# Low parts of the weights: stored to device memory at their first use, loaded from there at the second

## The chip, the cores and the metric

The kernel runs on one core of one Trainium2 chip. The metric is the time of one execution on the device in microseconds (us); lower is better. A core has five engines that run side by side, each with its own queue worked off in order: TensorE (PE, matrix products; its weight loads are shown apart as PEld), VectorE (DVE), ScalarE (ACT), GpSimd (POOL) and SyncE (SP), which here issues all DMA transfers. An instruction that waits holds up everything behind it in its engine's queue.

## The reference, cut to what matters

A decoder trunk of two layers works on a sequence of 1024 tokens with 1024 channels. In each layer the normalized input goes through one wide projection whose columns feed four mixers (a sparse attention, a gated spatial unit, a convolution module, a linear recurrence); their results go through an output projection, are normalized and added to the stream, and then a gated embedding is added:

```python
for i in range(DEPTH):
    h = rms_norm(x, g_pre[i])
    proj = h @ w_in[i]                      # 1024 x 3532, split among the mixers
    ...
    mix = concatenate([y_a * silu(z_a), y_b * silu(z_b), y_c * silu(z_c), y_d * silu(z_d)])
    x = x + rms_norm(mix @ w_out[i], g_post[i])
    x = x + sigmoid(x @ ple_gate[i]) * (p[i] @ ple_proj[i])
```

All is in float32. What the change touches are the four weight matrices `w_in`, `w_out`, `ple_gate` and `ple_proj`, which every token is multiplied with.

## The kernel before, in words

**Products in three parts.** Float32 products are made from a rounded format (`F32R`). A weight and an activation are each split into a high part (the value rounded to that format) and a low part (what the rounding left over); `mm3` (L161 to L165) then makes three products, high x high (L163), high x low (L164) and low x high (L165).

**Granules.** The weights stream through SBUF in granules of at most 128 x 512 numbers (256 KB). `w_granule` (L167) names the rows and columns, and `split_w` (L149) does the work: SP loads the raw numbers into a buffer `ws` (L154), ACT rounds them into `wh` (L157), and POOL subtracts the two into `wl` (L158). `ws`, `wh` and `wl` have three buffers each. There are 388 granules in the whole program; PE works 12 matrix products on most of them, 6 on a few.

**Halves.** The sequence is worked in two halves of 512 tokens (`h` 0 and 1) within each layer (`l` 0 and 1). Each half streams the layer's weights anew, so most granules are loaded and split twice. The string `ORDER` lists the steps of each (layer, half): `F`, `N`, `G`, `a` to `d` and `s` stream `w_in`, `O` streams `w_out` of the half before, `g` its `ple_gate`, `e` streams `ple_proj`; `R` and `r` are the recurrence, `A` a tile of attention, `T` the 31 convolution taps on DVE (L688). The granules number 64, 96, 96 and 132 in the four (layer, half) stages in program order; the last has the tail with it. `tail` (from L1134) ends the program for the last half: it cuts `w_out` and half of `ple_gate` into other granules than the steps `O` and `g` do.

**What sets the order.** The framework plans the program when it is built: it simulates the engines with its own costs and due times, fills each engine's queue in the order that comes out, and adds the semaphore waits. `split_w` runs under a raised priority (`high_priority(offset=4000)`), so that granules are fetched as early as their three buffers allow. A buffer is given to the next tile when the last instruction that uses it has ended.

Other transfers on the same SP queue: `x` for the norm (L270), `ped` stores of the embedding's product (L1069), loads of the spilled mixer results (`ld`, L1047), the recurrence's scratch (`Nd`, `Xd`, L453 to L530), `nsa_w1` (L858), and the output (`out_dram`, L1132).

Of the kernel before, what the change touches and what calls it, by code (L numbers as in the profile page):

```python
# [8 lines left out]
F32 = mybir.dt.float32  # L9
# [32 lines left out]
class Trunk:  # L42
    def __init__(self, ctx, tc, a):
        self.ctx, self.tc, self.nc, self.a = ctx, tc, tc.nc, a
        nc = self.nc
        self.dram = ctx.enter_context(tc.tile_pool(name="dram", bufs=1, space=bass.MemoryType.DRAM))
        self.cp = ctx.enter_context(tc.tile_pool(name="consts", bufs=1))
        self.sb = ctx.enter_context(tc.tile_pool(name="sb", bufs=1))
        self.pp = ctx.enter_context(tc.tile_pool(name="pp", bufs=1, space=bass.MemoryType.PSUM))
        self.n = 0  # L50
        self.nd, self.wide, self.xq, self.xs = 0, None, None, None
        self.setup()

    BUFS = {"aT": 16, "ws": 3, "wh": 3, "wl": 3, "t2": 7, "y": 7, "rv": 2, "pt": 4, "r4": 2, "ab": 8,
# [91 lines left out]
        nc.vector.tensor_copy(self.TC[:, :, 53:70], pj[:, :68].rearrange("p (a b) -> p a b", a=4))  # L146


    def split_w(self, src, cols):  # L149
        nc = self.nc  # L150
        with self.tc.high_priority(offset=4000):
            st = self.t([128, 512], "ws")
            for ap, w in src:
                nc.sync.dma_start(ap(st), w)  # L154
            hi = self.t([128, 512], "wh", dt=F32R)
            lo = self.t([128, 512], "wl", dt=F32R)
            nc.scalar.copy(hi[:, :cols], st[:, :cols])  # L157
            nc.gpsimd.tensor_sub(lo[:, :cols], st[:, :cols], hi[:, :cols].bitcast(F32))  # L158
        return hi, lo

    def mm3(self, out, lh, ll, rh, rl, first, last, shared=False):  # L161
# [5 lines left out]
    def w_granule(self, w2d, k0, nk, segs):  # L167
        n = sum(s[1] for s in segs)
        src = []
        o = 0  # L170
        for c0, cn in segs:
            def dst(st, o=o, cn=cn):
                return st[:, :nk * n].rearrange("p (k c) -> p k c", k=nk)[:, :, o:o + cn]
            src.append((dst, w2d[k0 * 128:(k0 + nk) * 128, c0:c0 + cn].rearrange("(k p) c -> p k c", p=128)))
            o += cn
        hi, lo = self.split_w(src, nk * n)
        v = lambda x: x[:, :nk * n].rearrange("p (k c) -> p k c", k=nk)
        return v(hi), v(lo)

# [1135 lines left out]
```

## Time and profile before

| | us |
|---|---|
| median of three runs | 1914.52 (1913.43 to 1916.66) |
| the profiled execution | 1914.54 |
| its span, first to last instruction | 1912.8 |
| mean granted TensorE clock | 0.94 |

Busy time of the engines over that span: PE 1709.7 us, DVE 1399.5, ACT 812.3, POOL 615.7. A busy PE is not PE at its peak, because matrix products are pipelined and their ends are modelled. The 16 DMA engines moved 182.28 MB.

A group's row reads: line, engine, operation, tile written <- tiles read, shapes, count | busy time, mean ns of one | idle time of the engine just before, and what ended most of it. A row of waits reads: who waited <- for whom: us in total, times, longest.

### The profile page before, as it was taken

The page shows a single profiled execution, that of the slowest core. Times are in us where ns is not written, and L with a number is a line of the kernel's source. Part 1 is how long each engine was busy: PE and PEld are TensorE (multiplying, and loading weights), DVE is VectorE, ACT ScalarE, POOL GpSimd, SP SyncE. Part 2 cuts the span into 40 slices and gives each one's busy share as a digit, 9 for nine tenths or more (in the row PEclk, how much of TensorE's full clock was granted, in tenths as well). Part 3 has the DMA queues.
Part 4 walks back from the last instruction along what each step waited for, and adds up shares of the span by engine and source line. Part 5 has one row for each costly group of instructions (what it writes and reads, how often), then busy time and mean ns, then how long its engine had stood idle before and what let it go on. Part 6 is the DMA issues. An engine that isn't in the chain of part 4 may idle for free. (4 is left out here: it accounts for less than half of the span.)

```text
span 1912.8 us, 27837 instructions
## 1 busy us (share of the span) xinstructions
PE 1709.7 (89%) x9444; PEld 1271.0 (66%) x9444; DVE 1399.5 (73%) x3457; ACT 812.3 (42%) x1837; POOL 615.7 (32%) x487
## 2 busy tenths in 40 slices
PE   5897988999789999989988989989979989979998
PEld 4565666666576676766666667766756767756677
DVE  4449987888897957777599881878789877476554
ACT  4332233544233455545322344545422435544543
POOL 2222333122342343312233346322233413412243
PEclk8798998899998999989999899999989979989999
DMA  6435332123532234422352243532253213223344
GB/s 212 87 87 108 79 102 77 45 53 64 118 82 78 79 93 135 126 72 55 74 125 68 68 139 96 175 111 55 67 102 86 70 45 116 62 88 108 114 142 149
DMA packets 326406, 182.28 MB, mean 95 GB/s; under 512 B 88556, under 2 KB 299504, under 8 KB 326264
## 3 DMA queue, kind: packets, MB, share of 16 engines
q1 hardware_dynamic: 326264, 180.51, 34.7%
q8 instruction: 74, 1.21, 0.3%
q14 instruction: 68, 0.56, 0.1%
HBM read 150.01 MB, written 30.44 MB: 94 GB/s over the span
## 5 line engine op out<-in xcount | busy, mean ns | idle before, releaser
L158 POOL TENSOR_TENSOR wl<-ws,wh 128x512 fp32r<-128x512 f32 (+2 forms) x388 | 524.2, 1353 | 1160.6 <-ACT wh L157 1010.7
L163 PE MATMUL mm<-aT,wh 128*128 128x512 f32 (+1 forms) x1304 | 540.6, 417 | 14.9 <-DVE y L653 6.6
L164 PE MATMUL mm<-aT,wh 128*128 128x512 f32 (+1 forms) x1304 | 537.0, 412 | 4.9 <-DVE aT L252 4.8
L165 PE MATMUL mm<-aT,wl 128*128 128x512 f32 (+1 forms) x1304 | 535.7, 411 | 0.0
L157 ACT CAST wh<-ws 128x512 fp32r<-128x512 f32 (+2 forms) x388 | 237.1, 612 | 483.7 <-PE mm L164 231.2
L163 PEld LDWEIGHTS mm<-aT,wh 128*128 128x128 f32 (+1 forms) x1304 | 251.9, 194 | 68.4 <-DVE y L653 7.5
L164 PEld LDWEIGHTS mm<-aT,wh 128*128 128x128 f32 (+1 forms) x1304 | 252.6, 194 | 56.1 <-DVE aT L252 11.5
L165 PEld LDWEIGHTS mm<-aT,wl 128*128 128x128 f32 (+1 forms) x1304 | 251.6, 193 | 49.0 <-issue 3.1
L688 DVE SCALAR_TENSOR_TENSOR cv<-cv,cw,cv 128x512 f32<-128x512 f32 x240 | 225.6, 955 | 3.5
L966 DVE TENSOR_TENSOR pt<-pt,pt 128x512 fp32r<-128x512 f32 (+1 forms) x152 | 93.8, 617 | 97.1 <-ACT pt L965 93.5
L1029 ACT ACTIVATE r<-s,sma 128x512 f32<-128x512 f32 (+3 forms) x192 | 106.0, 554 | 102.8 <-DVE sma L1027 65.9
L965 ACT CAST pt<-pt 128x512 fp32r<-128x512 f32 (+1 forms) x152 | 80.2, 527 | 121.0 <-PE pt L962 120.6
L962 PE MATMUL pt<-cst,r 128*128 128x128 f32 x528 | 99.7, 287 | 21.8 <-DVE r L1034 16.6
L962 PEld LDWEIGHTS pt<-cst,r 128*128 128x128 f32 x528 | 65.3, 145 | 51.5 <-DVE r L1034 31.0
L972 PE MATMUL pv<-pt,vs 128*128 128x256 f32 x264 | 81.6, 326 | 15.7 <-DVE pt L966 14.9
L971 PE MATMUL pv<-pt,vs 128*128 128x256 f32 x264 | 86.0, 326 | 5.1 <-ACT pt L965 4.9
L999 PE MATMUL s<-kv,qs 128*128 128x512 f32 (+2 forms) x192 | 76.9, 401 | 7.9 <-ACT r L1029 7.6
L1019 DVE CUSTOM_DVE_ANT_0 s<-s,T 128x256 f32<-128x256 f32 (+1 forms) x144 | 54.0, 376 | 40.9 <-PE s L1000 40.3
L972 PEld LDWEIGHTS pv<-pt,vs 128*128 128x128 f32 x264 | 52.0, 197 | 42.8 <-DVE pt L966 36.3
L1034 DVE TENSOR_SCALAR r<-r,sma 128x640 f32<-128x640 f32 (+7 forms) x128 | 78.4, 612 | 0.8
L971 PEld LDWEIGHTS pv<-pt,vs 128*128 128x128 f32 x264 | 51.8, 196 | 36.6 <-ACT pt L965 30.5
L1000 PE MATMUL s<-kv,qs 128*128 128x512 f32 (+2 forms) x192 | 66.2, 348 | 0.0
(337 smaller groups left out, 2831.8 us busy)
## 6 DMA issues: line engine op xcount, KB each, us to landing
ws<-in_w_in_dram SPq DMA_DIRECT2D x232, 256.0 KB, 2.9
ws<-in_ple_gate_dram SPq DMA_DIRECT2D x64, 256.0 KB, 2.9
ws<-in_w_out_dram SPq DMA_DIRECT2D x60, 256.0 KB, 2.8
ped<-ot SPq DMA_DIRECT2D x32, 256.0 KB, 3.5
ld<-in_nsa_w_dram SPq DMA_DIRECT2D x32, 256.0 KB, 3.4
ld<-ped SPq DMA_DIRECT2D x32, 256.0 KB, 3.1
mixd<-y SPq DMA_DIRECT2D x30, 256.0 KB, 2.1
ld<-mixd SPq DMA_DIRECT2D x30, 256.0 KB, 2.8
```

Source lines behind the costliest of these rows:

```text
L157: nc.scalar.copy(hi[:, :cols], st[:, :cols])
L158: nc.gpsimd.tensor_sub(lo[:, :cols], st[:, :cols], hi[:, :cols].bitcast(F32))
L163: nc.tensor.matmul(out, lh, rh, start=first, stop=False, skip_group_check=shared)
L164: nc.tensor.matmul(out, lh, rl, start=False, stop=False, skip_group_check=shared)
L165: nc.tensor.matmul(out, ll, rh, start=False, stop=last, skip_group_check=shared)
L688: nc.vector.scalar_tensor_tensor(ac, xg[j][:, k:k + TH], cw[:, j * 31 + k:j * 31 + k + 1], ac, op0=OP.mult, op1=OP.add)
L962: nc.tensor.transpose(pt[:, o:o + 128], P[e][:, (b + x - b0) * 128:(b + x - b0) * 128 + 128], self.ident)
L965: nc.scalar.copy(Th[:, :n], pt[:, :n])
L966: nc.vector.tensor_sub(Tl[:, :n], pt[:, :n], Th[:, :n].bitcast(F32))
L971: nc.tensor.matmul(acc, vs, Th[:, x * 256:x * 256 + 256], start=False, stop=False)
L972: nc.tensor.matmul(acc, vs, Tl[:, x * 256:x * 256 + 256], start=False, stop=last)
L1029: nc.scalar.activation(P[:, o:o + wd], p[:, c:c + wd], AF.Exp, bias=ng[:, 0:1], accum_out=den[:, x:x + 1])
```

## The change

`split_w` is given a key for its granule: the matrix's name and offset, the first row block, the number of row blocks and the columns. When the key comes for the first time, the low part is made as before and SP then stores it into a tile of device memory that is kept under the key. When the key comes again, POOL makes nothing, and SP loads the low part from that tile into `wl`. The raw weights are loaded and rounded in both cases. In the second case only ACT reads `ws`. A key that comes again within the same half counts too (`V0` in step `s` is streamed twice).

```diff
+        self.low = {}
...
-    def split_w(self, src, cols):
+    def split_w(self, src, cols, key):
...
             lo = self.t([128, 512], "wl", dt=F32R)
+            kept = self.low.get(key)
+            if kept is not None:
+                nc.sync.dma_start(lo[:, :cols].bitcast(F32), kept)
             nc.scalar.copy(hi[:, :cols], st[:, :cols])
-            nc.gpsimd.tensor_sub(lo[:, :cols], st[:, :cols], hi[:, :cols].bitcast(F32))
+            if kept is None:
+                nc.gpsimd.tensor_sub(lo[:, :cols], st[:, :cols], hi[:, :cols].bitcast(F32))
+                kept = self.low[key] = self.dram.tile([128, cols], F32, name=f"low{len(self.low)}")
+                nc.sync.dma_start(kept, lo[:, :cols].bitcast(F32))
         return hi, lo
...
-        hi, lo = self.split_w(src, nk * n)
+        hi, lo = self.split_w(src, nk * n, (w2d.tensor.name, w2d.offset, k0, nk, tuple(segs)))
```

## Rows read from the trace of the kernel before

**Rows 1.** The page, busy us of each engine, share of the span, instructions.
```profile
PE 1709.7 (89%) x9444; PEld 1271.0 (66%) x9444; DVE 1399.5 (73%) x3457; ACT 812.3 (42%) x1837; POOL 615.7 (32%) x487
```
**Rows 2.** The page's costliest groups, the subtraction.
```profile
L158 POOL TENSOR_TENSOR wl<-ws,wh 128x512 fp32r<-128x512 f32 (+2 forms) x388 | 524.2, 1353 | 1160.6 <-ACT wh L157 1010.7
```
**Rows 3.** The view of line L158, who waited for it: us, times.
```profile
  PEld mm L165: 0.8, 1
```
**Rows 4.** Waits of PE, 320 to 825 us, then 1265 to 1913 us.
```profile
PE pv L972 <- DVE pt L966: 9.4, 15, 2.0
...
PE pt L962 <- DVE sma L912: 0.9, 1, 0.9
...
PE pt L962 <- DVE r L1034: 8.0, 12, 1.8
...
PE pv L951 <- DVE tm L975: 1.0, 1, 1.0
```
**Rows 5.** The page, chain that ended last, by engine.
```profile
PE 15%; DVE 9%; issue 2%; ACT 2%; DMA 1%; POOL 0%; SPq 0%; ACTq 0%; DVEq 0%; POOLq 0%
```
**Rows 6.** Timeline, 1005 to 1008 us: start, duration, engine, line.
```profile
1005.19 1.48 POOL L158 TENSOR_TENSOR wl<-ws,wh 128x512 fp32r<-128x512 f32 x1 [4.93 <-PE mm L165]
...
1006.05 1.17 DVE L688 SCALAR_TENSOR_TENSOR cv<-cv,cw,cv 128x512 f32<-128x512 f32 x1
...
1007.68 0.74 DVE L688 SCALAR_TENSOR_TENSOR cv<-cv,cw,cv 128x512 f32<-128x512 f32 x1
```
**Rows 7.** Groups of DVE by form.
```profile
L688 DVE SCALAR_TENSOR_TENSOR cv<-cv,cw,cv 128x512 f32<-128x512 f32 x240 | 225.6, 955 | 3.5
...
L615 DVE SCALAR_TENSOR_TENSOR SB<-c,gc,q 64x64 f32<-64x64 f32 x112 | 31.7, 283 | 7.8 <-PE c L606 6.2
L913 DVE TENSOR_TENSOR sma<-sma,gate 128x1 f32<-128x1 f32 x128 | 27.6, 216 | 0.7
```
**Rows 8.** Views of three DVE lines: shortest/middle/longest ns, first and last start.
```profile
L688 DVE SCALAR_TENSOR_TENSOR cv<-cv,cw,cv x240: 681/752/1872, 179.9 to 1584.4; 128x512 f32<-128x512 f32 x120
...
L913 DVE TENSOR_TENSOR sma<-sma,gate x128: 141/154/1262, 291.5 to 1805.2; 128x1 f32<-128x1 f32 x128
...
L653 DVE SCALAR_TENSOR_TENSOR y<-y,mm x32: 669/681/690, 203.2 to 1603.6; 128x512 f32<-128x512 f32 x32
```
**Rows 9.** The view of tile `ws`: its loads on SP, ns, and their landing.
```profile
L154 SPq DMA_DIRECT2D ws<-in_w_in_dram x248: 367/368/1421, 8.6 to 1579.4; - x124
...
DMA to landing us min/median/max: 2.1/2.9/4.9
```
**Rows 10.** Timeline of POOL, 1871 to 1890 us.
```profile
1876.02 1.29 POOL L158 TENSOR_TENSOR wl<-ws,wh 128x512 fp32r<-128x512 f32 x1 [1.43 <-ACT wh L157]
1878.74 1.29 POOL L158 TENSOR_TENSOR wl<-ws,wh 128x512 fp32r<-128x512 f32 x1 [1.43 <-ACT wh L157]
```
**Rows 11.** Waits of SP's queue, whole span.
```profile
SPq L154 <- POOL wl L158: 1049.3, 360, 13.2
...
SPq L1132 <- ACT ot L1131: 21.7, 9, 5.5
```
**Rows 12.** The page, DMA issues: count, KB each, us to landing.
```profile
ped<-ot SPq DMA_DIRECT2D x32, 256.0 KB, 3.5
```
**Rows 13.** Timeline of SP, 0 to 60 us.
```profile
19.09 1.62 SPq L1069 DMA_DIRECT2D ped<-ot  x3
```
**Rows 14.** Timeline of PE, 24 to 28 us.
```profile
25.38 0.80 PE L163 MATMUL mm<-t,wh 128*128 128x512 f32 x1 [6.56 <-ACT ot L1068]
```
**Rows 15.** Windows of 10 us: busy us of each engine, clock, DMA share, GB/s.
```profile
0.00:10.00 10.00, 0.27 (x1) 0.28 (x1) 3.84 (x22) 4.04 (x6) 5.27 (x11) 1.00 0.78 230
...
20.00:30.00 10.00, 4.62 (x11) 3.66 (x12) 2.08 (x3) 4.03 (x7) 0.83 (x1) 0.69 0.85 303
```
**Rows 16.** The page, DMA queues: packets, MB, share of 16 engines.
```profile
q1 hardware_dynamic: 326264, 180.51, 34.7%
```
**Rows 17.** Waits of PE for DMA, whole span.
```profile
PE pt L861 <- DMA ld<-in_nsa_w_dram: 10.8, 9, 2.8
PE rp L534 <- DMA x<-Xd: 8.2, 8, 3.4
```

## The prediction

> **What bounds the kernel now.** I read the page first: PE is busy for 1709.7 of 1912.8 us, DVE for 1399.5, POOL for 615.7 [rows 1]. So TensorE's stream of matrix products sets the time, and what can still be gained is its 203 us of idle time. The costliest single group is the subtraction that makes the low parts, 388 times 1353 ns on POOL [rows 2]; but POOL idles 1160.6 us in front of it, waiting for the rounded copy from ACT. The question is then who waits for that subtraction. The view of its line answers: PE, once, for 0.8 us [rows 3]. As a supplier of weights it is off the path, and taking it away shortens nothing directly.
>
> The waits of PE say what does stand in its way. In the two stretches where most of the loads will fall (320 to 825 us and 1265 to 1913 us), the waits that a DVE instruction ended add up to 24.5 us (8 lines) and 40.1 us (13 lines) [rows 4]. The chain of waits says the same: DVE 9% of the span, POOL 0% [rows 5]. It reaches back only as far as its shares sum, 29% or 555 us. So the indirect way counts: does POOL's subtraction slow DVE? Three rows show it [rows 6]. A convolution tap takes 0.74 us alone and 1.17 us when it meets a subtraction. Over all 240 taps the mean is 955 ns, with 752 in the middle and 1872 at most [rows 7, 8]. So the taps alone lose about 240 x (0.955 - 0.745) = 50 us. A tiny product of 128x1 shows it too: median 154 ns, longest 1262, mean 216. An instruction that takes one operand from PSUM does not: L653 stays between 669 and 690 ns. I did this for all 149 forms of DVE instruction that occur both with and without POOL beside them, with the median of the undisturbed ones as the measure; L688 gives the most, L615 the least (nothing) [rows 7]. The sum is 177 us, 12.7% of DVE's busy time.
>
> **The change part by part.** Who stores and who loads follows from the key in the code. A granule's first use stores, every later one loads. By stage (layer, half) the loads are 4 of 64 granules, 64 of 96, 36 of 96 and 72 of 132: 176 loads and 212 stores. Of the stores 52 are never read, since the tail cuts its matrices otherwise and the last layer's output weights have no second use in the same cut.
>
> *Removed: 176 subtractions.* 176 x 1.353 = 238 us of POOL, nothing of it on the path. DVE gets back 176/388 of 177 us, about 80 us. What of it reaches the end: on the chain, DVE's 172 us (9%) contain 12.7% of such delay, 22 us; half of the granules in that stretch are loaded ones (59 of 119), so 11 us, and for all 176 loads 11 x 176/59 = 33 us. That is the upper end, since the chain ignores what comes second; the lower end is 0. I take 14 us, under half: PE's waits for DVE last 0.5 to 1 us each [rows 4], and behind most of them an ACT copy or PE's own queue is next.
>
> The Trainium skill (SBUF - State Buffer, Who interferes with whom) says that DVE with two SBUF inputs and a GpSimd instruction that reads SBUF exclude each other for the whole instruction, and that DMA contends with no engine. If DVE stood waiting through every removed subtraction, an estimate by that rule would give back 238 us of DVE; the rows give 80, because often DVE has an operand in PSUM or POOL is the one that waits.
>
> *Added: 176 loads of the low part.* One takes 0.37 us to issue and 2.9 us to land (at most 4.9) [rows 9]. It can be issued only when PE is done with the granule three before, because there are three buffers. In the densest stretch subtractions follow each other every 2.72 us, 1878.74 - 1876.02 [rows 10], which is PE's pace for a granule. From the free buffer to the first use there lie two granules, 5.4 us, and the load needs 0.37 + 2.9 = 3.3. So it is hidden with 2.1 us to spare, and elsewhere, where PE takes 4 to 5 us for a granule, with more. Without that cover each would cost up to 3.3 us.
>
> *Added: 212 stores.* Each stands in SP's queue behind a wait for its subtraction. SP waits there already: the weight loads wait 1049.3 us in 360 waits for the same subtraction [rows 11], since it frees their buffer. The store needs its 0.37 us and then lands in about 3.5 us like the stores of `ped` [rows 12], while PE comes to the granule only later; the buffer is free in time. Cost on the path: 0 in the middle of the kernel.
>
> *The edges.* At the start it isn't hidden. SP issues the stores of `ped` at 19.09 us [rows 13], PE waits 6.56 us until 25.38 for an ACT copy that needs the buffers of these stores [rows 14], and the DMA engines are 0.78 to 0.85 busy at up to 303 GB/s [rows 15]. Four stores of low parts come before: 4 x 0.4 = 1.6 us of issue at least, 4 x 256 KB at 303 GB/s = 3.5 us at most. I take 2.5. At the end the last low loads stand in one queue with the stores of the output, which wait 21.7 us in 9 waits for ACT, 5.5 at most [rows 11]: 0 to 5.5, I take 1.5, below the mean wait of 2.4, since only some of the last loads meet one.
>
> *Other transfers.* The 388 DMAs are about 100 MB on top of 180.5, so the DMA engines go from 34.7% to 54% busy if a byte costs the same [rows 16]. PE waits 10.8 us for `nsa_w1` and 8.2 us for `Xd` [rows 17]. If these grew by the share of added traffic (100/180) it would be 10 us, at least 0; I take 3, since most stretches have idle engines.
>
> *Sum*: -14 + 2.5 + 1.5 + 3 = -7 us. The profiled execution took 1914.54 us (span 1912.8 and 1.7 around it), as good as the median of the runs, 1914.52. Forecast 1907.5 us.
>
> **Rivals.** *It stays hidden.* The 80 us of DVE come back where DVE isn't late, or another engine takes the place; the edges cost 4 and are just paid for: 1911 to 1918, say 1914.5. For it: POOL 0% and PE 89% busy. Against it: PE's waits for DVE.
>
> *The load of the low part becomes the late one (slower).* Before, SP was three loads ahead and POOL, which waits for nobody but ACT, made the low part. Now SP itself must be on time at the moment when PE frees the buffer; whatever stands before it in SP's queue (a store waiting for DVE or ACT, a load without a buffer) delays it, and behind it wait the next raw weights and the transfers of the recurrence. It decides from 2.1 us of lateness in the dense stretches. If one load in four misses by 0.5 us, that is 44 x 0.5 = 22 us, and the sum becomes +15: 1929.5. For it: single waits of SP of 5 to 13 us [rows 11]. Against it: most granules have more cover than the densest.
>
> *The planner's order.* The order on every engine is worked out at build time from the planner's own estimates, and the swap of a subtraction for a DMA moves its due times. The trace cannot price that; by a tenth of PE's idle 203 us it is 20 us either way: 1888 or 1928.
>
> *Full relief*: the 33 us of the chain with only the edges to pay: 1914.5 - 33 + 4 = 1885.5.
>
> **How the numbers follow.** Forecast 0.40, with its own range 1898 to 1910; hidden 0.22; the late load 0.22; the planner 0.10 (0.06 slower, 0.04 faster); full relief 0.06. A difference under 0.2% (3.8 us) can't be told from none here. Faster: 0.40 + 0.04 + 0.06 = 0.50; same 0.22; slower 0.22 + 0.06 = 0.28. The range 1890 to 1931 leaves out full relief and the worst of the late load.
>
> **What would show it.** Right: L158 has 212 instructions and some 290 us busy; DVE busy falls by about 80 us with the same count, and the taps' mean falls where the loads are; PE's waits for DVE shrink in 320 to 825 and 1265 to 1913 us; the first matrix product of the second half of `embed` starts 2 to 3 us later than 25.4 us; PE waits nowhere for a DMA into `wl`. Wrong: lines "PE waits for DMA wl" or ACT casts that wait for DMA `ws` of over 10 us in sum (the late load), a DVE busy time that does not fall (no relief), or the same DVE relief with PE's idle time unchanged (hidden).

## The result, and the profile after

The changed kernel takes 1894.13 us (median of 4 runs, 1884.96 to 1898.52) against 1913.97 us before; the ratio is 0.9889, interval 0.985 to 0.9927. That is 20 us faster, where 7 were forecast. The profiled execution is the longest of the four: 1898.52 us, with a span of 1896.8.

The page of the changed kernel: busy times, the DMA queue, the subtraction's group, and the two DMA issues that are new (count, KB, us to landing).

```profile
PE 1692.2 (89%) x9444; PEld 1267.9 (67%) x9444; DVE 1306.3 (69%) x3457; ACT 813.4 (43%) x1837; POOL 375.9 (20%) x311
...
q1 hardware_dynamic: 382136, 280.34, 50.6%
...
L163 POOL TENSOR_TENSOR wl<-ws,wh 128x512 fp32r<-128x512 f32 (+1 forms) x212 | 282.9, 1336 | 697.1 <-ACT wh L161 599.3
...
low<-wl SPq DMA_DIRECT2D x200, 256.0 KB, 2.1
wl<-low SPq DMA_DIRECT2D x172, 256.0 KB, 2.8
```

Beside [rows 1, 2 and 16]: 212 subtractions are left, POOL loses 240 us, and DVE, which has not one instruction less (3457), loses 93 us of busy time. The groups by form of three DVE lines, which answer to [rows 7] (the taps are now L695, the product with an operand in PSUM L622, the small one L920):

```profile
L695 DVE SCALAR_TENSOR_TENSOR cv<-cv,cw,cv 128x512 f32<-128x512 f32 x240 | 191.9, 815 | 3.3
...
L622 DVE SCALAR_TENSOR_TENSOR SB<-c,gc,q 64x64 f32<-64x64 f32 x112 | 31.7, 283 | 10.5 <-PE c L613 7.0 <-ACT wh L161 1.5 <-ACT pc L940 0.4
L920 DVE TENSOR_TENSOR sma<-sma,gate 128x1 f32<-128x1 f32 x128 | 22.8, 178 | 0.5
```

The taps fall from 955 to 815 ns on average; the view of their line still has 748 ns in the middle and 1872 at most, as in [rows 8], since 212 of the 388 subtractions remain. The instruction with an operand in PSUM keeps its 283 ns.

PE's waits for DVE in the two stretches of [rows 4] (us, times, longest), and its waits for DMAs over the span, the longest of which answers to [rows 17]:

```profile
PE pv L979 <- DVE pt L973: 5.3, 8, 2.6
PE pt L969 <- DVE r L1041: 2.3, 5, 1.0
...
PE rp L575 <- DVE xf L551: 0.3, 1, 0.3
```
```profile
PE pt L969 <- DVE r L1041: 4.7, 8, 1.4
PE rp L648 <- DVE yt L644: 2.2, 1, 2.2
...
PE rp L448 <- DVE q L466: 0.7, 1, 0.7
```
```profile
PE pt L868 <- DMA ld<-in_nsa_w_dram: 63.8, 12, 11.6
...
PE mm L172 <- DMA wl<-low: 1.1, 1, 1.1
```

The 10 lines of the first stretch add up to 12.6 us, the 11 of the second to 20.0. Before, they were 28.6 (16 lines) and 42.5 (19 lines); the prediction's 24.5 and 40.1 are sums of the longest lines alone. Both are less than half of what they were. For the loads of the low parts PE waits 2.0 us in three waits, the longest 1.1. But the wait for `nsa_w1` is 63.8 us instead of 10.8. Where it comes from is seen in SP's timeline, 176 to 193 us, and in PE's (start, duration, engine, line; in brackets the idle time before it):

```profile
176.30 0.50 SPq L165 DMA_DIRECT2D low<-wl  x1
176.90 0.40 SPq L155 DMA_DIRECT2D ws<-in_w_in_dram  x1
177.35 1.82 SPq L497 DMA_DIRECT2D Xd<-q  x3
179.27 0.48 SPq L865 DMA_DIRECT2D ld<-in_nsa_w_dram  x1
187.40 3.90 SPq L497 DMA_DIRECT2D Xd<-q  x8
191.40 0.95 SPq L865 DMA_DIRECT2D ld<-in_nsa_w_dram  x2
```
```profile
182.38 0.65 PE L868 MATMUL pt<-ld,t 128*32 128x128 f32 x8 [10.78 <-DMA ld<-in_nsa_w_dram]
194.36 0.66 PE L868 MATMUL pt<-ld,t 128*32 128x128 f32 x8 [11.33 <-DMA ld<-in_nsa_w_dram]
```

The loads of `nsa_w1` stand in SP's queue behind the writes of `Xd`, and PE stands still for 11 us twice. Ahead of the loads that end the second stop, from 179.75 to 187.40 us, the queue waits for a DVE result that a write of `Xd` needs, and not for a store:

```profile
SPq L497 <- DVE q L509: 7.6, 1, 7.6
```

In the kernel before, the same loads were issued ahead of and among those writes:

```profile
150.90 0.45 SPq L858 DMA_DIRECT2D ld<-in_nsa_w_dram  x1
...
152.13 0.50 SPq L858 DMA_DIRECT2D ld<-in_nsa_w_dram  x1
157.16 3.59 SPq L490 DMA_DIRECT2D Xd<-q  x5
...
161.33 1.57 SPq L490 DMA_DIRECT2D Xd<-q  x3
...
163.53 0.46 SPq L858 DMA_DIRECT2D ld<-in_nsa_w_dram  x1
```

So the change has a gain and a loss, each larger than the sum. The durations of the four (layer, half) stages, from the first product of a stage's first granule to that of the next (the first from the start of the span, the last to its end), show the two apart; the last two lines are what PE idles in each:

```
stage              1      2      3      4    (us)
loads/stores    4/60  64/32  36/60  72/60
before         339.6  505.6  433.5  634.1
after          361.2  483.9  444.6  607.0
difference     +21.6  -21.7  +11.1  -27.1
PE idle before  60.3   42.8   37.5   62.5
PE idle after   77.7   32.1   51.4   43.5
```

The halves that mostly store get longer, those that mostly load get shorter, and PE's idle time goes the same way. Its sum hides this: 203.1 us before, 204.6 after.

### The profile page after: what moved, and what is told of

It is laid out like the page before. It is cut to its first block, busy times and chain, and to the rows that moved or that the text cites. A ratio compares the mean times of both kernels' runs of the same rounds, so it can differ in the third digit from the quotient of the medians.

```text
span 1896.8 us, 28498 instructions
## 1 busy us (share of the span) xinstructions
PE 1692.2 (89%) x9444; PEld 1267.9 (67%) x9444; DVE 1306.3 (69%) x3457; ACT 813.4 (43%) x1837; POOL 375.9 (20%) x311
## 3 DMA queue, kind: packets, MB, share of 16 engines
q1 hardware_dynamic: 382136, 280.34, 50.6%
## 5 line engine op out<-in xcount | busy, mean ns | idle before, releaser
L163 POOL TENSOR_TENSOR wl<-ws,wh 128x512 fp32r<-128x512 f32 (+1 forms) x212 | 282.9, 1336 | 697.1 <-ACT wh L161 599.3
L695 DVE SCALAR_TENSOR_TENSOR cv<-cv,cw,cv 128x512 f32<-128x512 f32 x240 | 191.9, 815 | 3.3
L609 POOL TENSOR_TENSOR q<-SB,gc 128x256 f32<-128x256 f32 x28 | 24.4, 871 | 431.3 <-DMA Xd<-q 152.3
L1006 PE MATMUL s<-kv,qs 128*128 128x512 f32 (+2 forms) x192 | 77.1, 402 | 6.1 <-ACT r L1036 5.8
L1041 DVE TENSOR_SCALAR r<-r,sma 128x640 f32<-128x640 f32 (+7 forms) x128 | 72.2, 564 | 0.9
L868 PE MATMUL pt<-ld,t 128*32 128x128 f32 x256 | 12.8, 325 | 64.6 <-DMA ld<-in_nsa_w_dram 63.8
```

Source lines behind the costliest of these rows:

```text
L695: nc.vector.scalar_tensor_tensor(ac, xg[j][:, k:k + TH], cw[:, j * 31 + k:j * 31 + k + 1], ac, op0=OP.mult, op1=OP.add)
```

## The experiments

The theory: the gain is DVE's relief from POOL's subtraction, and the stores take part of it back. The rivals: the gain comes from POOL's freed time (the low part is ready earlier, or ACT and SP are released earlier); the loads are late; the planner's order alone moves the time. Each result is a ratio to the kernel before, run beside it; the last column is the ratio's distance from 1, times 1914 us.

```
kernel                                 ratio   95% interval    us
after                                  0.9889  0.985  0.9927   -21
E1 subtractions put back               1.0172  1.0157 1.0187   +33
E2 stores only, nothing loaded         1.0166  1.0134 1.0198   +32
E3 loads only, one store               0.964   0.9623 0.9657   -69
E4 nsa_w1 loaded earlier               0.9967  0.9946 0.9988    -6
B4 the kernel before, with the same    0.9891  0.9864 0.9918   -21
E5 no low part at the second use       0.9632  0.9596 0.9668   -70
E6 memsets in the subtraction's place  0.9938  0.9915 0.9961   -12
E8 stores issued by POOL               0.9813  0.9778 0.9848   -36
X1 stores of a sixteenth               0.9781  0.9737 0.9825   -42
X2 store at plain priority             0.9781  0.9752 0.981    -42
X4 four low buffers                    1.0022  0.9995 1.0048    +4
X6 as X2, only stores that are read    0.978   0.9752 0.9808   -42
```

**E1: the 176 subtractions put back**, into a buffer that nobody reads afterwards; loads and stores stay.

```diff
             nc.scalar.copy(hi[:, :cols], st[:, :cols])
+            if kept is not None:
+                nc.gpsimd.tensor_sub(st[:, :cols], st[:, :cols], hi[:, :cols].bitcast(F32))
```

> The changed kernel, with the subtraction on POOL kept at a granule's second use as well, its result thrown away into the raw buffer; stores and loads stay. Relief theory (the gain is DVE no longer held up by POOL; PE's idle time ended by DVE fell from 117 to 65 us): that gain goes, the costs of the stores and loads stay, 1925 to 1950 us, DVE busy back at 1380 to 1400 us. Rival (the gain comes from the planner's other order or from earlier prefetch): it stays near 1894 us whatever POOL does.

```profile
PE 1699.8 (87%) x9444; PEld 1265.2 (65%) x9444; DVE 1388.8 (71%) x3457; ACT 814.5 (42%) x1837; POOL 613.8 (31%) x487
...
L697 DVE SCALAR_TENSOR_TENSOR cv<-cv,cw,cv 128x512 f32<-128x512 f32 x240 | 220.7, 934 | 3.3
```

DVE's busy time rises by 82.5 us, the taps to 934 ns, and the kernel loses the whole gain and 33 us more. Against the changed kernel the subtractions cost 1.0172 - 0.9889 = 2.8%, 54 us.

**E6: two memsets of 128x512 in the place of each such subtraction.** They wait for the same copy, hold the same raw buffer and keep POOL nearly as busy (561.2 us against 613.8 in E1), but only write. They don't read `wh`, and so don't hold it from ACT as the subtraction does.

```diff
+            if kept is not None:
+                for _ in range(2):
+                    nc.gpsimd.memset(st[:, :cols], 0.0)
```

> The changed kernel with, at a granule's second use, two POOL memsets of the raw buffer in the place where the subtraction was: POOL writes the buffer but reads nothing, behind the same wait for ACT, and the buffer comes free behind it. Relief theory in the form 'DVE is held up while POOL reads': 1890 to 1905 us, as without the subtraction, and DVE busy near 1306 us. Rival (what costs is POOL's queue, standing behind ACT and PE, or the later release of the raw buffer): near the run with the subtraction kept, 1954 us.

```profile
L164 POOL MEMSET ws<- 128x512 f32 (+1 forms) x352 | 186.3, 530 | 506.9 <-ACT wh L161 494.4 <-issue 2.4
...
L698 DVE SCALAR_TENSOR_TENSOR cv<-cv,cw,cv 128x512 f32<-128x512 f32 x240 | 191.9, 814 | 3.3
```

POOL is 185 us busier than in the changed kernel, and the taps keep their 814 ns. Of the 54 us of E1 only 0.9938 - 0.9889 = 0.5%, 9 us, return, with intervals that overlap; POOL's occupation, the longer hold of the raw buffer and a new order cost about that much together. One rival E6 leaves out: ACT waits 30.7 us for the subtractions that E1 puts back, and never for the memsets. But PE's waits for ACT add up to 56.1 us in E1, 56.7 in E6 and 52.2 in the changed kernel, and those for DVE to 98.2, 64.0 and 63.7: most of what the subtraction adds to PE's waits, DVE ends. So the rest of the 54 us is put down to what the subtraction does to DVE. The Trainium skill (SBUF - State Buffer, Who interferes with whom) says that a DVE instruction with two SBUF inputs contends with a GpSimd instruction that reads SBUF, and not with one that only writes it; these two traces agree (934 against 814 ns).

**E2: stores only**; every use subtracts, as before. **E3: loads only**; one low part is stored, once, and every second use loads that one.

```diff
 (E2)
-            if kept is not None:
-                nc.sync.dma_start(lo[:, :cols].bitcast(F32), kept)
...
-            if kept is None:
-                nc.gpsimd.tensor_sub(lo[:, :cols], st[:, :cols], hi[:, :cols].bitcast(F32))
+            nc.gpsimd.tensor_sub(lo[:, :cols], st[:, :cols], hi[:, :cols].bitcast(F32))
+            if kept is None:
 (E3)
-                kept = self.low[key] = self.dram.tile([128, cols], F32, name=f"low{len(self.low)}")
-                nc.sync.dma_start(kept, lo[:, :cols].bitcast(F32))
+                if not self.low:
+                    self.low0 = self.dram.tile([128, 512], F32, name="low0")
+                    nc.sync.dma_start(self.low0, lo.bitcast(F32))
+                self.low[key] = self.low0[:, :cols]
```

> First use stores the low part; the second use subtracts as before and loads nothing, so the stores are never read. If the stores make the nsa_w1 loads and the start late (PE waited 64 us for nsa_w1 in the changed kernel, 11 before): 1930 to 1955 us, with PE's wait for nsa_w1 at 40 us or more. If the loads do it, or both only together: 1914 to 1920 us.

> No stores but one: every second use loads the low part of the first granule of all, the same 256 KB each time, so the low products are those of other weights. If the stores are the cost and the relief the gain: 1850 to 1875 us, PE's wait for nsa_w1 near 11 us. If the loads are the cost: 1885 to 1900 us, as in the changed kernel.

**E5: no traffic at all**: neither stores nor loads nor, at the second use, subtractions; the high part stands in for the low one.

```diff
-            lo = self.t([128, 512], "wl", dt=F32R)
...
-            if kept is not None:
-                nc.sync.dma_start(lo[:, :cols].bitcast(F32), kept)
+            lo = hi if kept else self.t([128, 512], "wl", dt=F32R)
...
-                kept = self.low[key] = self.dram.tile([128, cols], F32, name=f"low{len(self.low)}")
-                nc.sync.dma_start(kept, lo[:, :cols].bitcast(F32))
+                self.low[key] = True
```

> No store, no load, and no subtraction at a granule's second use, where the high part takes the place of the low one in the third product. The relief alone, without any traffic. Relief theory: 1850 to 1875 us, DVE busy near 1300 us, within 10 us of the run with loads only, since those are hidden. Rival (the loads are late): clearly below the run with loads only, by 15 us or more. Rival (POOL was not the cause): 1905 to 1915 us.

The busy times of E3, then of E5, and PE's wait for `nsa_w1` in E2, then in E3:

```profile
PE 1682.9 (91%) x9444; PEld 1262.8 (68%) x9444; DVE 1315.6 (71%) x3457; ACT 813.4 (44%) x1837; POOL 382.7 (21%) x311
```
```profile
PE 1688.5 (91%) x9444; PEld 1269.5 (69%) x9444; DVE 1317.6 (71%) x3457; ACT 812.1 (44%) x1837; POOL 377.5 (20%) x311
```
```profile
PE pt L866 <- DMA ld<-in_nsa_w_dram: 47.7, 11, 11.9
```
```profile
PE pt L870 <- DMA ld<-in_nsa_w_dram: 26.0, 10, 11.0
```

The stores alone cost 32 us, and their presence beside the loads 0.9889 - 0.964 = 2.5%, 48 us. The loads cost nothing that shows: E3 with 176 loads and E5 without one lie within 0.1%, and so do E1 and E2, which both store and subtract at every use and of which only E1 loads. That is the end of the rival of late loads. Without any stores the relief comes to 69 us, by E1 to 54; each is one pair of kernels, with a new order in it, so these are two estimates and not bounds.

The stages of the profiled executions, one of each kernel, show where the prices are paid:

```
stage              1      2      3      4    (us)
loads/stores    4/60  64/32  36/60  72/60
E1             363.1  511.0  452.9  625.1
E2             366.4  509.3  443.1  631.9
E3             340.1  482.8  429.2  600.7
E4             366.0  476.8  438.5  631.4
```

Over the changed kernel, E1's subtractions cost 2, 27, 8 and 18 us, most in the two stages that load most. Over the kernel before, E2's stores cost 27, 4, 10 and -2 us, although stages 1, 3 and 4 store 60 granules each. So the stores have no fixed price apiece; why it differs so by stage isn't shown.

**E4 and B4: the loads of `nsa_w1` earlier**, in the changed kernel and in the kernel before.

```diff
-                w = self.t([128, TH], "ld")
-                nc.sync.dma_start(w.rearrange("p (l m) -> p l m", l=4),
...
+                with self.tc.high_priority(offset=1000):
+                    w = self.t([128, TH], "ld")
+                    nc.sync.dma_start(w.rearrange("p (l m) -> p l m", l=4),
...
```

> The changed kernel with the eight loads of nsa_w1 in each stage at a raised priority (offset 1000). If the cost of the stores is that these loads come late behind the recurrence's transfers in SP's queue: PE's wait for them falls from 64 us to under 15, time 1845 to 1865 us. If the late loads are only where a delay shows that the stores cause anyway: 1880 to 1895 us, and the wait appears elsewhere.

> The kernel before with the same raised priority of the nsa_w1 loads and nothing else. PE waited 11 us for them there, so at most that is to be had: 1900 to 1921 us. If it gains much more, the raised priority does something else than end that wait, and the run of the changed kernel with it tells less.

PE's waits in E4:

```profile
PE mm L170 <- ACT ot L1076: 15.6, 3, 10.0
PE rp L648 <- DVE yt L644: 14.6, 8, 3.9
PE rp L548 <- DVE q L544: 12.4, 7, 4.3
...
PE pt L869 <- DMA ld<-in_nsa_w_dram: 2.8, 3, 1.5
```

The wait is gone, 64 us to 2.8, and the kernel is no faster: 15 us slower than the changed one, above both ranges that were expected. Most of the time waited stands in other lines now: PE's waits for DVE rise from 63.7 to 100.9 us (L648 from 9.3 to 14.6), those for ACT from 52.2 to 64.4. So most of the 64 us were where a delay showed, not what it cost. The 15 us themselves don't stand in PE's waits: its idle time is 197.7 us, 7 less than in the changed kernel, and its busy time 1715.0, 22.8 more for the same 9444 products. By stage (the table above), E4 is 5 us longer than the changed kernel in stage 1, 7 and 6 shorter in stages 2 and 3, and 24 longer in stage 4, where the wait had been 8.3 us. What lengthens stage 4 stays open. In the kernel before, the same edit gains 21 us, although this wait had 10.8 us to give and keeps 7.3 of them:

```profile
PE pt L862 <- DMA ld<-in_nsa_w_dram: 7.3, 7, 2.4
```

One edit, 21 us faster on one kernel and 15 slower on the other, and in both far from what its wait had to give. What it moves beside that wait is the order that the planner makes on every engine; by this reading an order is worth as much as the change itself. It isn't shown apart from the rest: the mean granted clock was 0.944 to 0.954 in B4's four runs and 0.935 to 0.945 in those of the kernel before, and how much of the 21 us goes with it isn't separated.

**E8, X1, X2: what it is about the stores.** E8 issues them from POOL, right behind the subtraction, so that SP's queue has none. X1 writes 32 columns of each low part (and loads one whole low part everywhere, as E3). X2 leaves bytes and queue and moves the store out of the block of high priority, so that SP may issue it later.

```diff
 (E8)
-                nc.sync.dma_start(kept, lo[:, :cols].bitcast(F32))
+                nc.gpsimd.dma_start(kept, lo[:, :cols].bitcast(F32))
 (X1, beside E3's edit)
+                part = self.dram.tile([128, 32], F32, name=f"part{len(self.low)}")
+                nc.sync.dma_start(part, lo[:, :32].bitcast(F32))
 (X2)
-                kept = self.low[key] = self.dram.tile([128, cols], F32, name=f"low{len(self.low)}")
-                nc.sync.dma_start(kept, lo[:, :cols].bitcast(F32))
+        if kept is None:
+            kept = self.low[key] = self.dram.tile([128, cols], F32, name=f"low{len(self.low)}")
+            nc.sync.dma_start(kept, lo[:, :cols].bitcast(F32))
```

> The changed kernel with the 212 stores issued from POOL's queue, where the subtraction has just ended, and not from SP's. If the stores cost by standing in SP's queue behind their wait for POOL: 1850 to 1870 us, PE's wait for nsa_w1 under 25 us. If they cost by their bytes or by holding the buffer: 1885 to 1900 us. If issuing from POOL itself is slow: above 1900 us, POOL busy well over 376 us.

> The changed kernel with stores of 32 columns only (16 KB, not 256) and every load reading one tile that is stored whole once, as in the run with loads only. As many stores, at the same place in SP's queue, with a sixteenth of the bytes and soon landed. If the stores cost by standing in SP's queue: 1880 to 1900 us, as the changed kernel. If by their bytes or by holding the low buffer until they have landed: 1850 to 1865 us, as with loads only.

> The changed kernel with the stores at ordinary priority, so that the planner puts them behind transfers of the recurrence and of nsa_w1 that are due earlier. If a store that waits for POOL at the head of SP's queue is what costs: 1855 to 1880 us and PE's wait for nsa_w1 under 30 us. If bytes or buffers cost: 1885 to 1900 us. If the low buffer is now held too long: above 1900 us, with POOL waiting for DMA.

E8's page, the store's group and its landing; then SP's timeline in X2, 165 to 172 us:

```profile
L165 POOL DMA_DIRECT2D low<-wl x212 | 120.4, 568 | 81.2 <-POOL wl L163 79.6
...
low<-wl POOLq DMA_DIRECT2D x200, 256.0 KB, 3.4
```
```profile
165.06 4.20 SPq L498 DMA_DIRECT2D Xd<-q  x8
169.36 0.44 SPq L866 DMA_DIRECT2D ld<-in_nsa_w_dram  x1
169.84 1.50 SPq L166 DMA_DIRECT2D low<-wl  x3
```

Each of X1 (between its two expected ranges) and X2 wins back 21 of the 48 us, X1 with a sixteenth of the bytes written, X2 with all of them in a place behind the writes of `Xd`. PE's wait for `nsa_w1` falls to 37.9 and 30.2 us. E8 wins 15 and pays 120 us of POOL, 568 ns for each issue. So neither the bytes nor the place in SP's queue explain the price alone.

**X6: X2 without the 52 stores that nobody reads** (`again` is false for their keys); 160 stores and 176 loads remain.

```diff
-                kept = self.low[key] = self.dram.tile([128, cols], F32, name=f"low{len(self.low)}")
-                nc.sync.dma_start(kept, lo[:, :cols].bitcast(F32))
+        if kept is None and again:
+            kept = self.low[key] = self.dram.tile([128, cols], F32, name=f"low{len(self.low)}")
+            nc.sync.dma_start(kept, lo[:, :cols].bitcast(F32))
```

> The changed kernel with the stores at ordinary priority and the 52 stores that are never read left out (last layer's w_out, what the tail cuts otherwise, the last half's ple_gate): 160 stores, 176 loads, the same result. With the stores at ordinary priority alone it was 1875 us. If each store costs its share of the 42 us between the changed kernel and loads only (212 stores, 0.2 us each): 1862 to 1872 us. If the cost sits at the recurrence in the first halves, where all stores stay: 1870 to 1880 us, no better.

It measures the same as X2. A quarter of the stores costs nothing where it stood. But all 52 stood in stage 4 (60 stores there in X2, 8 in X6), where E2's stores cost nothing either; X6 says nothing of the stores in stages 1 and 3. X2 and X6 are faster than both kernels: 2.2% under the one before.

**X4: four buffers for the low part** instead of three (`"wl": 4`, and `"smc"` 6 instead of 8 to make room).

> The changed kernel with four buffers for the low part in place of three (room made by taking two of eight small buffers of the norms). If the stores cost because they hold the low buffer and so keep POOL from the next subtraction, or the loads because they wait for a buffer: 1860 to 1880 us. If the place in SP's queue or the bytes cost: 1885 to 1900 us.

25 us slower than the changed kernel and above both expected ranges, with the same DVE relief (1316.2 us busy). More room for the stores is no cure; with two buffers less for small tiles and a new order in the same edit, it settles nothing else.

## Why the prediction was right, and what was mis-sized

The sign held, the first half of the mechanism (DVE is relieved), and the wide range, 1890 to 1931; the forecast's own range, 1898 to 1910, just missed the 1894.13. The two large terms of the sum were each far too small, and the errors nearly cancelled: that the time came out 13 us from the forecast was luck.

*The relief: 14 us forecast, 54 to 69 measured (E1 against the changed kernel; E3).* The first half of the step held: DVE's busy time fell by 93 us (80 forecast), and E1 and E6 show that the subtraction is the cause and POOL's being busy isn't. The second half, what reaches the end, failed, and its "upper end" of 33 us too. It was taken from a chain of waits that covered 555 of 1913 us, as if DVE's delay counted only where the chain passes through DVE. The idle time of PE that DVE ended fell, over the whole span, from 117 to 65 us (summed over PE's gaps): 52 us. Most of these waits are short (114.8 us in 135 waits before, 0.85 us on average), which the prediction took as a reason to halve. The rival of full relief, with 0.06, came nearest to this term. So two thirds (54 of 82.5 us, E1) to four fifths (69 of 84, E3) of what DVE got back reached the end, where the prediction let a sixth of its 80 through.

*The stores: "Cost on the path: 0 in the middle of the kernel"; measured 32 (E2) to 48 us (changed kernel against E3).* This is the other step that failed. It asked whether SP may wait there, since it did so before [rows 11]. The waits of SP's queue in the changed kernel (the store is L165, the load of the low part L160, that of the raw weights L155) show that it waits no longer than before:

```profile
SPq L165 <- POOL wl L163: 535.7, 194, 12.8
SPq L160 <- PE mm L172: 294.1, 136, 12.0
...
SPq L155 <- ACT wh L161: 37.2, 48, 5.0
```

The sum of the three is 867 us, against 1049.3 for one. What the step did not ask is what stands behind the waiting store: with the store placed at high priority the planner put the loads of `nsa_w1` behind it and behind the writes of `Xd`, and X2, where only the store's place differs in the code, wins 21 us back, most of it in stages 1 and 3 (11 us each in the profiled executions). The stores don't make all of that wait: with one store (E3) it is still 26.0 us, against 10.8 before. And that the late loads are the price isn't shown, since E4 ended the wait and gained nothing. The prediction's own term for such transfers was 3 us.

*The loads: hidden.* Right: 2.0 us of PE's waits, and E3 equals E5. The rival of late loads, with 0.22, is refuted, although its sign appears to the letter: ACT's casts wait 35.0 us for raw weights, where 10 was the limit. They waited 17.1 us in the kernel before and 26.1 in E5, which loads no low part at all, so the limit told nothing.

*The edges: 2.5 us at the start.* Twice that. SP's first stores go out at 8.35 us, ahead of the next weight loads, the stores of `ped` follow at 23.22 instead of 19.09 us, and PE starts the second half of `embed` at 30.34:

```profile
30.34 0.80 PE L170 MATMUL mm<-t,wh 128*128 128x512 f32 x1 [10.31 <-ACT ot L1075]
```

against 25.38 in [rows 14], 5.0 us later. The tail's 1.5 us can't be told from the rest.

*The sign for "hidden".* "The same DVE relief with PE's idle time unchanged" also came true to the letter, 203.1 and 204.6 us. The stages show that it means something else here: idle time fell by 30 us in stages 2 and 4 and rose by 31 in stages 1 and 3. A sum over the span can't tell no effect from two that cancel.

*Who waited for the subtraction.* [rows 3] shows PE alone. The same view has a line above it:

```profile
  ACT wh L157: 102.0, 52
```

So POOL held up ACT too, and the prediction left that way out. It isn't where the gain comes from: PE's waits for ACT are 51.7 us before and 52.2 after.

*The planner's order: 20 us either way.* B4 (-21 us) and E4 (+15), the same edit, suggest its size with both signs. With 0.10 it was then given too little: it is as large as the net result, and how much of the net result is such an order can't be told. For that reason no difference below some 20 us between two kernels with different orders, as between E8 and X2, can be put down to its edit alone; the 21 us of X1 and of X2 lie on that border.

*What stays open.* How much of the stores' price is the wait in SP's queue, how much the bytes (the DMA engines go from 34.7 to 50.6% busy), and how much the order. Nor does the trace explain PE's busy time, which fell by 17.5 us for the same 9444 products (10.9 and 8.1 less in stages 2 and 4) while its idle time stayed at 203 to 205 us (52 less for DVE, 53 more for `nsa_w1`); the ends of the products are modelled, and the granted clock was no higher (0.93 against 0.94). The clock differs between the kernels, too: 0.930 to 0.938 in the runs of the changed kernel, 0.928 to 0.933 in E1's, 0.943 to 0.948 in E3's. Whether it follows the waits or adds to them, these runs don't separate.

## What to carry to other kernels

An engine that the bound engine doesn't wait for can still cost its time through the engine that it slows: compare an instruction's mean with its undisturbed middle before calling a line hidden, and price the delay over all waits of the bound engine, not along one chain. Compare by stage as well: over the span, PE's idle time hid both terms here. Before a DMA that waits for a computation goes into a queue in order, list what stands behind it there; its own landing time says nothing on that. And where a planner orders the work at build time, an edit of no consequence is needed beside the real one, to see what a new order is worth by itself.

## What was not expected of the hardware

POOL's memsets of 530 ns leave DVE's taps at 814 ns, its subtractions of 1361 ns in the same place raise them to 934. A DMA issued by POOL takes 568 ns of POOL's time, the same one on SP 0.32 us in the middle (the view of the store's line in the changed kernel). Its landing takes 3.4 us there and 2.1 from SP in the changed kernel, but 3.3 from SP in X2; so the issuer isn't shown to be the reason.
